# One matmul instead of three between the sixth and the seventh product of a Strassen step

## The chip, the cores and the metric

The kernel runs on one core of a Trainium2 chip. The metric is the time of one execution in microseconds (us) on the device. Three runs of the kernel before took 2034.97, 2035.05 and 2035.65 us, so the median is 2035.05 us. One further execution was profiled; the trace and all views quoted below are of that one.

## The reference

The program is a decoder trunk of two layers over 256 positions and 2048 channels, in float32:

```python
for l in range(DEPTH):                                   # 2
    h = rms_norm(x, norm1_g[l])
    z = h @ w_in[l]                                      # 2048 x 5120
    q, k, v, gu, gv = jnp.split(z, splits, axis=-1)
    attn = dilated_attention(rotary(q), rotary(k), v)    # 8 heads
    gm = chunked_gmlp(gelu(gu), gelu(gv), ...)           # 8 groups
    x = x + concatenate([attn, gm]) @ w_out[l]           # 2048 x 2048
    h2 = rms_norm(x, norm2_g[l])
    x = x + square(relu(h2 @ w_up[l])) @ w_down[l]       # 2048 x 8192 x 2048
return rms_norm(x, final_g)
```

The change lies in the last product, `w_down`, and in the steps that stand among its own.

## The kernel before, in words

**Precision.** Every large product is made of three matmuls in a float32 form with a short mantissa. A weight block `raw` is split into `hi` (a rounded copy, made by ScalarE, L167) and `lo` (what the rounding left, `raw - hi`, made by VectorE, L177). The activations are split the same way. A product is then `hi*xh + lo*xh + hi*xl`. So a block of weights can be used by its first matmul once ScalarE has made `hi`, and by its second once VectorE has made `lo`.

**Steps.** The work is a list of steps, and each consumes one or more weight blocks of 128 x 1024 numbers. There are three kinds:

- `natural`: the activations are the stationary operand and 512 weight columns stream (lines 459 to 461).
- `transposed`, the channel-major step: the weights are stationary and 256 positions stream. One step is one block: 2 column halves times 4 row blocks times the three matmuls of lines 400 (`hi`, `xh`), 402 (`lo`, `xh`) and 404 (`hi`, `xl`), so 24 matmuls. Its output goes to a PSUM bank `acc`.
- `fast`, the seven-product step: a Strassen-like multiplication of 2 x 2 blocks with seven products in place of eight, used on a part of `w_down`. Here 128 x 128 pieces of the activations (`half`, or their sums in `shared`) are stationary and 256 weight columns stream. A product is 2 times the three matmuls of lines 430 (`hi`), 432 (`lo`) and 433 (`hi` with the low part of the activations), so 6 matmuls. A step takes four blocks, two of the weights themselves (`Top`, `Bottom`) and two of their sums (`Sums`, first `upper`, then `lower`); the sums are made by VectorE in four subtractions (L218, L219, L222, L223), and then these blocks are split into `hi` and `lo` as the others are. The last `lo` of the four is that of `lower`.

**The seventh product.** The step issues six products and puts the seventh into the list `left_over`. The next step is always a `transposed` one. Within it, ahead of the second row block, the seventh product is taken from the list and issued: so behind the first three matmuls of that step. It writes its own half of a PSUM bank `aux`. It uses the `lower` block, which the sixth product has used already, and the activations in `half`.

**Order.** The program is written step by step and the order on each engine is the order of the code. Before the matmuls of a step the loop at the end of the kernel writes the `hi` of later blocks for ScalarE, the due pieces of earlier results, the `lo` of later blocks for VectorE, and the loads. VectorE works in that order too, so its `lo` for one step stands behind the sums, the other splits and the accumulations written ahead of it.

**How often.** For each of the eighths `e = 1` to `7` of the hidden width, the tables `ORDER` and `USUAL` give the places of two or three column groups of 512, each with two seven-product steps: 2 + 3 + 3 + 3 + 3 + 3 + 2 = 19 groups in a layer, 38 steps, and 76 in both layers. So there are 76 places at which a seventh product is issued inside a `transposed` step.

Of the kernel before, what the change touches and what calls it, by code (L numbers as in the profile page):

```python
# [90 lines left out]
def trunk(ctx: ExitStack, tc: tile.TileContext, layout, xT, consts, gains, w, b_sp, w_sp, out):  # L91
# [42 lines left out]
    def acc_bank(i=None, of=4):  # L134

        if i is None:
            i = bank_at[0] = (bank_at[0] + 1) % of
        return pacc.tile([P, 512], F32, name=f"acc{i}", tag=f"acc{i}")
# [217 lines left out]
    left_over = []  # L356
# [12 lines left out]
    def transposed(name, l, row0, nk, col0, ncols, moving, after, between=None, apart=False, of=4, cols=None):  # L369

        cols = cols or range(0, ncols, 256)
        order = [(c, k) for c in cols for k in range(0, nk, 4)]
        if between:
            h = nk // 8
            order[h:2 * h], order[2 * h:3 * h] = order[2 * h:3 * h], order[h:2 * h]  # L380
        accs = {}
        for n, (c, k0) in enumerate(order):
            if between and n == nk // 4:
                mark(between)
            wt = Sub(name, l, row0 + k0 * P, col0 + c, 4, 256)

            def mm(wt=wt, k0=k0, c=c):
                two = apart and c == cols[-1]
                if k0 == 0:
                    accs[c] = [acc_bank(of=of), acc_bank(of=of)] if two else acc_bank(of=of)  # L390
                ps = accs[c]
                for cb in range(2):
                    o = ps[cb][:, 0:S] if two else ps[:, cb * S:(cb + 1) * S]
                    for k in range(4):
                        if cb == 0 and k == 1 and left_over:
                            left_over.pop()()
                        xs = moving(k0 + k)
                        hi = wt.hi[:, k, cb * P:(cb + 1) * P]
                        last = k0 + k == nk - 1
                        pe.matmul(o, lhsT=hi, rhs=xs[:, 0, :], start=(k0 + k == 0 and (two or cb == 0)), stop=False,  # L400
                                  skip_group_check=True)
                        pe.matmul(o, lhsT=wt.lo[:, k, cb * P:(cb + 1) * P], rhs=xs[:, 0, :], start=False, stop=False,  # L402
                                  skip_group_check=True)
                        pe.matmul(o, lhsT=hi, rhs=xs[:, 1, :], start=False, stop=last, skip_group_check=True)  # L404
            steps.append((wt, mm, (lambda c=c: after(c, accs[c])) if k0 + 4 == nk else None))
# [58 lines left out]
    def mark(fn):  # L464

        steps.append((None, fn, None))
# [601 lines left out]
```

## Time and profile before

| | before |
|---|---|
| median of three runs | 2035.05 us (2034.97 to 2035.65) |
| profiled execution, first to last instruction (its span) | 2033.3 us |
| TensorE matmul busy | 2018.3 us (99%), 16834 matmuls |
| VectorE busy | 1577.6 us (78%) |
| ScalarE busy | 1213.4 us (60%) |
| granted TensorE clock, mean | 0.997 |

The profile gives no other time for the profiled execution than its span; the median of the runs is 1.75 us longer than the span, for what lies ahead of the first and behind the last instruction.

How to read the rows that follow. In a row of the timeline stand the start, the duration, the engine, the line, the operation and the tiles (written `out<-in`). PE is TensorE's matmul, PEld its weight load, DVE is VectorE, ACT is ScalarE. Matmuls are pipelined: each lasts about 0.28 us in the records and the next begins about 0.113 us after it, so what counts is the distance from one start to the next, not the duration. In a row of waits stand who waited for whom, the microseconds in total, how many times, and the longest.

### The profile page before, as it was taken

Reading aid. Unit: us, or ns where it says so; the run is one execution under the profiler, and the core shown is the slowest. Engines: PE = TensorE matmul, PEld = TensorE weight load, DVE = VectorE, ACT = ScalarE, POOL = GpSimd, SP = SyncE. Lnnn points to the kernel's source line nnn. Section 1 sums busy time; section 2 is a strip of 40 time slices with the busy share of each in tenths; the row PEclk is TensorE's granted clock in tenths of the full one; section 3 lists DMA queues with packets and bytes.
Section 4 is the critical chain, followed back from the end, with each engine's and each line's share of the span. In section 5 each row is a group of like instructions: output and inputs, shape, how many; then the busy total and the mean of one; then the engine's idle time right before and its main releaser. Section 6 shows DMA issues by size and latency. Waiting matters only on the chain.

```text
span 2033.3 us, 40721 instructions
## 1 busy us (share of the span) xinstructions
PE 2018.3 (99%) x16834; PEld 1979.1 (97%) x16834; DVE 1577.6 (78%) x1950; ACT 1213.4 (60%) x1613; POOL 156.7 (8%) x200
## 2 busy tenths in 40 slices
PE   9999999999999999999999999999999999999997
PEld 8998999999999999999989989999999999999997
DVE  7566766688888898998856667667888898888985
ACT  7565454666666666656545654556666666667654
POOL 0002300000001001100000032000000100010000
PEclk9999999999999999999999999999999999999998
DMA  8555556566677766875664555565676776778562
GB/s 326 192 167 166 187 187 205 169 232 209 211 228 236 244 218 201 243 222 198 204 214 159 169 184 187 187 203 179 215 223 213 230 234 217 230 221 261 184 213 81
DMA packets 126443, 419.27 MB, mean 206 GB/s; under 512 B 14128, under 2 KB 22064, under 8 KB 126256
## 3 DMA queue, kind: packets, MB, share of 16 engines
q1 hardware_dynamic: 110800, 389.86, 56.4%
q0 software_dynamic: 14304, 23.86, 6.7%
q8 instruction: 132, 2.16, 0.4%
q10 hardware_dynamic: 1152, 2.94, 0.4%
q14 instruction: 55, 0.45, 0.1%
HBM read 394.58 MB, written 22.02 MB: 205 GB/s over the span
## 4 chain that ended last, share of the span: by engine, by line
PE 95%; DVE 3%; ACT 1%; issue 1%; DMA 1%; ACTq 0%; DVEq 0%; SPq 0%
PE acc L402 23%; PE acc L400 23%; PE acc L404 23%; PE acc L461 3%; PE acc L460 3%; PE acc L459 3%; PE aux L430 3%; PE aux L432 3%; PE acc L433 3%; PE aux L433 3%; PE acc L432 3%; PE acc L430 3%; DVE lo L177 1%; ACT hi L167 1%; PE aux L693 0%
## 5 line engine op out<-in xcount | busy, mean ns | idle before, releaser
L167 ACT ACTIVATE hi<-raw 128x1024 fp32r<-128x1024 f32 (+1 forms) x817 | 836.2, 1051 | 497.9 <-DVE raw L219 231.2
L177 DVE TENSOR_TENSOR lo<-raw,hi 128x1024 fp32r<-128x1024 f32 (+1 forms) x817 | 964.1, 1213 | 155.1 <-ACT hi L167 151.7
L400 PE MATMUL acc<-hs,hi 128*128 128x256 f32 x2816 | 781.3, 277 | 0.0
L402 PE MATMUL acc<-hs,lo 128*128 128x256 f32 x2816 | 779.4, 277 | 0.2
L404 PE MATMUL acc<-hs,hi 128*128 128x256 f32 x2816 | 778.3, 276 | 0.0
L402 PEld LDWEIGHTS acc<-hs,lo 128*128 128x128 f32 x2816 | 528.7, 188 | 2.5 <-DVE lo L177 1.8
L400 PEld LDWEIGHTS acc<-hs,hi 128*128 128x128 f32 x2816 | 528.7, 188 | 0.3 <-issue 0.2
L404 PEld LDWEIGHTS acc<-hs,hi 128*128 128x128 f32 x2816 | 528.6, 188 | 0.0
L400 PE MATMUL acc<-half,hi 128*128 128x256 f32 x1344 | 372.1, 277 | 2.3 <-ACT hi L167 2.3
L402 PE MATMUL acc<-half,lo 128*128 128x256 f32 x1344 | 371.0, 276 | 0.0
L404 PE MATMUL acc<-half,hi 128*128 128x256 f32 x1344 | 371.0, 276 | 0.0
L400 PEld LDWEIGHTS acc<-half,hi 128*128 128x128 f32 x1344 | 252.3, 188 | 2.6 <-ACT hi L167 2.6
L402 PEld LDWEIGHTS acc<-half,lo 128*128 128x128 f32 x1344 | 252.3, 188 | 0.0
L404 PEld LDWEIGHTS acc<-half,hi 128*128 128x128 f32 x1344 | 252.2, 188 | 0.0
L866 POOL DMA_DIRECT2D far<-ar x92 | 74.7, 983 | 1159.9 <-ACT ar L869 607.0
L432 PE MATMUL acc<-lo,shared 128*128 128x256 f32 x384 | 106.4, 277 | 0.0
L433 PE MATMUL acc<-hi,shared 128*128 128x256 f32 x384 | 106.1, 276 | 0.0
L430 PE MATMUL acc<-hi,shared 128*128 128x256 f32 x384 | 106.1, 276 | 0.0
L459 PE MATMUL acc<-hi,hs 128*128 128x512 f32 x256 | 101.5, 397 | 0.1
L461 PE MATMUL acc<-hi,hs 128*128 128x512 f32 x256 | 100.6, 393 | 0.0
L460 PE MATMUL acc<-lo,hs 128*128 128x512 f32 x256 | 100.1, 391 | 0.3 <-DVE lo L177 0.3
L643 DVE TENSOR_TENSOR half<-ar,half 128x512 fp32r<-128x512 f32 x72 | 49.7, 691 | 62.1 <-ACT half L640 61.0
(163 smaller groups left out, 2560.2 us busy)
## 6 DMA issues: line engine op xcount, KB each, us to landing
raw<-in_w SPq DMA_DIRECT2D x731, 512.0 KB, 4.7
far<-ar POOLq DMA_DIRECT2D x60, 256.0 KB, 6.0
far<-ar POOLq DMA_DIRECT2D x32, 128.0 KB, 4.5
ar<-far POOLq DMA_DIRECT2D x12, 256.0 KB, 8.6
raw<-in_w SPq DMA_DIRECT2D x10, 256.0 KB, 5.2
x<-in_xT SPq DMA_DIRECT2D x7, 256.0 KB, 5.6
out<-x SPq DMA_DIRECT2D x7, 256.0 KB, 3.1
shared<-in_b_sp ACTq DMA_DIRECT2D x2, 512.0 KB, 7.8
```

The lines of the kernel that those rows point to most:

```text
L167: act.activation(self.h[:, j * m:(j + 1) * m], self.raw[:, j * m:(j + 1) * m], AF.Copy)
L177: vec.tensor_tensor(lo[:, r], self.raw[:, r], self.h[:, r].bitcast(F32), op=OP.subtract)
L400: pe.matmul(o, lhsT=hi, rhs=xs[:, 0, :], start=(k0 + k == 0 and (two or cb == 0)), stop=False, skip_group_check=True)
L402: pe.matmul(o, lhsT=wt.lo[:, k, cb * P:(cb + 1) * P], rhs=xs[:, 0, :], start=False, stop=False, skip_group_check=True)
L404: pe.matmul(o, lhsT=hi, rhs=xs[:, 1, :], start=False, stop=last, skip_group_check=True)
L430: pe.matmul(o[n], lhsT=xh, rhs=hi, start=(p == 0 and k == 0 and n in fresh), stop=False, skip_group_check=True)
L432: pe.matmul(o[n], lhsT=xh, rhs=lo, start=False, stop=False, skip_group_check=True)
L433: pe.matmul(o[n], lhsT=xl, rhs=hi, start=False, stop=(n in last and p == 1 and k == 1), skip_group_check=True)
L459: pe.matmul(ps, lhsT=xh, rhs=hi, start=(k0 + k == 0), stop=False)
L460: pe.matmul(ps, lhsT=xh, rhs=lo, start=False, stop=False)
L461: pe.matmul(ps, lhsT=xl, rhs=hi, start=False, stop=(k0 + k == KC - 1))
L866: nc.gpsimd.dma_start(far[g][:, r], src, **({} if e == max(g, 1) else {"accum_op": OP.add}))
```

## The change

The diff moves the two lines that take the seventh product from the list. They stood ahead of a row block's three matmuls, on condition that it is the second of the first half; they stand now behind the first of the three, wherever the list is not empty. As the list is filled by the step just before, that is the first matmul of the step.

```diff
                 for cb in range(2):
                     o = ps[cb][:, 0:S] if two else ps[:, cb * S:(cb + 1) * S]
                     for k in range(4):
-                        if cb == 0 and k == 1 and left_over:
-                            left_over.pop()()
                         xs = moving(k0 + k)
                         hi = wt.hi[:, k, cb * P:(cb + 1) * P]
                         last = k0 + k == nk - 1
                         pe.matmul(o, lhsT=hi, rhs=xs[:, 0, :], start=(k0 + k == 0 and (two or cb == 0)), stop=False,
                                   skip_group_check=True)
+                        if left_over:
+                            left_over.pop()()
                         pe.matmul(o, lhsT=wt.lo[:, k, cb * P:(cb + 1) * P], rhs=xs[:, 0, :], start=False, stop=False,
                                   skip_group_check=True)
                         pe.matmul(o, lhsT=hi, rhs=xs[:, 1, :], start=False, stop=last, skip_group_check=True)
```

With the two lines gone from above it, the first of the three matmuls moves from line 400 to line 398; 402 and 404 keep their numbers.

On TensorE, at the first of the 76 places (the end of the first seven-product step of `e = 1` in layer 0; `hi_4437` and `lo_4469` are the block of the `transposed` step, `hi_4407` and `lo_4439` that of `lower`), the order before is:

```order
L433 MATMUL aux_4475<-hi_4407,shared_4236 128x256
L400 MATMUL acc0_4382<-hs_85,hi_4437 128x256 [waits Activation_49]
L402 MATMUL acc0_4382<-hs_85,lo_4469 128x256 [waits DVE_49]
L404 MATMUL acc0_4382<-hs_85,hi_4437 128x256
L430 MATMUL aux_4476<-hi_4407,half_3857 128x256
L432 MATMUL aux_4476<-lo_4439,half_3857 128x256
L433 MATMUL aux_4476<-hi_4407,half_3857 128x256
L430 MATMUL aux_4476<-hi_4407,half_3857 128x256
L432 MATMUL aux_4476<-lo_4439,half_3857 128x256
L433 MATMUL aux_4476<-hi_4407,half_3857 128x256
L400 MATMUL acc0_4382<-hs_85,hi_4437 128x256
```

Now it is:

```order
L433 MATMUL aux_4475<-hi_4407,shared_4236 128x256
L398 MATMUL acc0_4382<-hs_85,hi_4437 128x256 [waits Activation_49]
L430 MATMUL aux_4476<-hi_4407,half_3857 128x256
L432 MATMUL aux_4476<-lo_4439,half_3857 128x256
L433 MATMUL aux_4476<-hi_4407,half_3857 128x256
L430 MATMUL aux_4476<-hi_4407,half_3857 128x256
L432 MATMUL aux_4476<-lo_4439,half_3857 128x256
L433 MATMUL aux_4476<-hi_4407,half_3857 128x256
L402 MATMUL acc0_4382<-hs_85,lo_4469 128x256 [waits DVE_49]
L404 MATMUL acc0_4382<-hs_85,hi_4437 128x256
L398 MATMUL acc0_4382<-hs_85,hi_4437 128x256
```

The six matmuls of the seventh product moved ahead of the step's second and third matmul. The wait for VectorE's `lo` went with the second matmul, six places back; the wait for ScalarE's `hi` stayed. The six themselves wait for nothing in either order.

The second place is the second seven-product step of the column group that the table puts at places 1 and 2 of `e = 6`, in layer 0 (`hi_9612` and `lo_9654` are the block of the `transposed` step, `hi_9610` and `lo_9616` that of `lower`). Before:

```order
L433 MATMUL acc0_9561<-hi_9610,shared_4236 128x256
L400 MATMUL acc1_9527<-hs_85,hi_9612 128x256 [waits Activation_49]
L402 MATMUL acc1_9527<-hs_85,lo_9654 128x256 [waits DVE_49]
L404 MATMUL acc1_9527<-hs_85,hi_9612 128x256
L430 MATMUL aux_4476<-hi_9610,half_8722 128x256
L432 MATMUL aux_4476<-lo_9616,half_8722 128x256
```

Now:

```order
L433 MATMUL acc0_9561<-hi_9610,shared_4236 128x256
L398 MATMUL acc1_9527<-hs_85,hi_9612 128x256 [waits Activation_49]
L430 MATMUL aux_4476<-hi_9610,half_8722 128x256
L432 MATMUL aux_4476<-lo_9616,half_8722 128x256
L433 MATMUL aux_4476<-hi_9610,half_8722 128x256
L430 MATMUL aux_4476<-hi_9610,half_8722 128x256
L432 MATMUL aux_4476<-lo_9616,half_8722 128x256
L433 MATMUL aux_4476<-hi_9610,half_8722 128x256
L402 MATMUL acc1_9527<-hs_85,lo_9654 128x256 [waits DVE_49]
```

It is the same move, and no wait is added or dropped. The orders of VectorE, ScalarE, GpSimd and SyncE are the same in both kernels, instruction for instruction, so no load and no store moves against them.

## Prediction

> **What bounds the kernel now.** I read the page first, then the waits of TensorE, then the order of time around the places that the change touches.
>
> ```profile
> span 2033.3 us, 40721 instructions
> PE 2018.3 (99%) x16834; PEld 1979.1 (97%) x16834; DVE 1577.6 (78%) x1950; ACT 1213.4 (60%) x1613; POOL 156.7 (8%) x200
> PEld acc L400 <- ACT hi L167: 2.6, 2, 1.3
> PEld acc L402 <- DVE lo L177: 1.8, 8, 0.3
> ```
>
> TensorE sets the time, and it hardly stands still. The last two rows are from the waits of its weight loads, with total, count and longest: in the whole span only 1.8 us go to a channel-major step's second matmul (L402) waiting for VectorE's `lo`. This is the wait that the change moves, so the gain cannot be large. Now the places in order of time, TensorE's matmuls alone:
>
> ```profile
> 802.22 0.28 PE L400 MATMUL acc<-hs,hi 128*128 128x256 f32 x1
> 802.51 0.39 PE L402 MATMUL acc<-hs,lo 128*128 128x256 f32 x1
> 802.73 0.28 PE L404 MATMUL acc<-hs,hi 128*128 128x256 f32 x1
> ...
> 808.26 0.28 PE L432 MATMUL acc<-lo,shared 128*128 128x256 f32 x1
> ...
> 810.27 0.28 PE L400 MATMUL acc<-hs,hi 128*128 128x256 f32 x1
> 810.60 0.39 PE L402 MATMUL acc<-hs,lo 128*128 128x256 f32 x1
> 810.83 0.28 PE L404 MATMUL acc<-hs,hi 128*128 128x256 f32 x1
> ...
> 893.05 0.28 PE L430 MATMUL acc<-hi,shared 128*128 128x256 f32 x1
> 893.22 0.39 PE L432 MATMUL acc<-lo,shared 128*128 128x256 f32 x1
> 893.45 0.28 PE L433 MATMUL acc<-hi,shared 128*128 128x256 f32 x1
> ...
> 924.31 0.28 PE L400 MATMUL acc<-hs,hi 128*128 128x256 f32 x1
> 924.54 0.39 PE L402 MATMUL acc<-hs,lo 128*128 128x256 f32 x1
> 924.76 0.28 PE L404 MATMUL acc<-hs,hi 128*128 128x256 f32 x1
> ...
> 1930.51 0.28 PE L400 MATMUL acc<-hs,hi 128*128 128x256 f32 x1
> 1930.73 0.39 PE L402 MATMUL acc<-hs,lo 128*128 128x256 f32 x1
> 1930.95 0.28 PE L404 MATMUL acc<-hs,hi 128*128 128x256 f32 x1
> ```
>
> From the first row of a triple to the third are two gaps, which take 0.23 us at the usual 0.113. They take 0.51 at 802, so 0.28 are lost there; 0.56 at 810, so 0.33; 0.45 at 924, so 0.22; 0.44 at 1930, so 0.21. I count ten such places in the trace: the pair 802 and 810 stands four times (twice in each layer, at the seven-product steps that follow each other closely in `e = 6` and in `e = 7`), and 924 and 1930 are the same step in the two layers. The triple at 893 is another wait, inside a seven-product step between the two of such a pair: 0.40 for two gaps, so 0.17 lost. The change does not touch that one.
>
> What VectorE does meanwhile:
>
> ```profile
> 800.10 2.35 DVE L177 TENSOR_TENSOR lo<-raw,hi 128x1024 fp32r<-128x1024 f32 x2
> 802.37 0.68 DVE L190 TENSOR_TENSOR lo<-raw,hi 128x512 fp32r<-128x512 f32 x1
> ...
> 806.28 0.69 DVE L223 TENSOR_TENSOR raw<-raw 128x512 f32<-128x512 f32 x1
> 806.89 4.79 DVE L177 TENSOR_TENSOR lo<-raw,hi 128x1024 fp32r<-128x1024 f32 x4
> ...
> 802.00:812.00 10.00, 9.50 (x11) 1.00 0.63 190
> ...
> 1951.78 0.69 DVE L782 SCALAR_TENSOR_TENSOR ar<-acc,nR 128x512 f32<-128x512 f32 x1 [3.12 <-PE acc L404]
> ```
>
> In the window from 802 to 812 it is busy 9.50 of 10.00 us (fifth row), without a pause until 806.89 + 4.79 = 811.68. In these stretches VectorE does not follow TensorE; it is late from its own queue. Outside them it does: the last row has it idle for 3.12 us until TensorE delivers, in layer 1 behind all 76 places, and a gain made before such a row is kept.
>
> **The ordinary place.** At the 66 others no wait is to be seen, but the pace is:
>
> ```profile
> 400.59 0.28 PE L433 MATMUL aux<-hi,shared 128*128 128x256 f32 x1
> 400.70 0.28 PE L400 MATMUL acc<-hs,hi 128*128 128x256 f32 x1
> 400.82 0.28 PE L402 MATMUL acc<-hs,lo 128*128 128x256 f32 x1
> 400.94 0.28 PE L404 MATMUL acc<-hs,hi 128*128 128x256 f32 x1
> 401.06 0.28 PE L430 MATMUL aux<-hi,half 128*128 128x256 f32 x1
> 401.18 0.28 PE L432 MATMUL aux<-lo,half 128*128 128x256 f32 x1
> ...
> 401.77 0.28 PE L400 MATMUL acc<-hs,hi 128*128 128x256 f32 x1
> 401.89 0.28 PE L402 MATMUL acc<-hs,lo 128*128 128x256 f32 x1
> ...
> 402.12 0.28 PE L400 MATMUL acc<-hs,hi 128*128 128x256 f32 x1
> ...
> L430 PE MATMUL aux<-hi,half x264: 276/280/283, 396.6 to 1931.4; 128*128 128x256 f32 x132
> L430 PE MATMUL aux<-hi,shared x224: 276/276/277, 398.0 to 1930.2; 128*128 128x256 f32 x112
> ```
>
> From 400.59 to 402.12 are 13 gaps, 1.53 us, where 13 x 0.1133 = 1.47 would do: about 0.057 lost. The gap into the step is normal (0.11). From the gap behind its first matmul on, each is 0.117 to 0.122, through the three matmuls, the six of the seventh product and two more. The last two rows, from the view of line 430 (shortest, median, longest ns), say that this is so everywhere: of the 264 matmuls on `aux` and `half` 152 are seventh products, and their group's median is 280 ns; where the same line runs deep inside a step (`aux` and `shared`) it is 276 with at most 277. So 76 x 0.057 = 4.3 us hang on changing between the two kinds of step.
>
> **The change, part by part.** No instruction is added or removed; on the other engines nothing moves. At each place six matmuls come ahead of two.
>
> *The moved wait.* Behind the waiting L402 stood the seventh product, which needs nothing new. It now covers the wait with six gaps, 6 x 0.113 = 0.68 us, more than the longest loss of 0.33. Behind the wait now stands only the rest of its own step. So at all ten places the stall there ends. What is late next:
>
> - At 924 and 1930 nothing close follows. Gain 0.22 + 0.21 = 0.43.
> - In a pair, the first stall's gain is not kept. TensorE would reach the seven-product step's wait 0.28 us earlier, at 893.22 in the second pair and 808.26 in the first. At 893 it waits already. At 808.26 the `lo` it needs is the first of the four that begin at 806.89, done at 806.89 + 4.79/4 = 808.09, and a weight load starts a gap ahead of its matmul, at 808.15: nothing to spare. As VectorE has no pause there, TensorE waits those 0.28 us at that place. Gain 0. If VectorE did move with TensorE, it would be the whole 4 x 0.28 = 1.1.
> - The second stall's gain is kept, since VectorE is through at 811.68. Gain 4 x 0.33 = 1.3.
>
> *The slow pace.* After 1930 it lasts longer than elsewhere:
>
> ```profile
> 925.50:930.50 5.00, 5.00 (x47) 1.00 0.87 304
> 1931.50:1936.50 5.00, 5.00 (x45) 1.00 0.87 281
> ```
>
> In equal 5 us two matmuls fewer are done in layer 1, at 0.113 about 0.2 us. It set in with the stall; without the stall I count it as gained: 0.2.
>
> At each place the stretch of slow gaps loses two members, since two matmuls of the step no longer stand between the first switch and the seventh product. At 0.005 each that is 0.010, times 76 = 0.8. The trace has no switch after a single matmul, so this has two ends: the stretch vanishes (0.057, gain 4.3), or it outlives the step (rival 2, loss). I take the value that goes by the rows as they are: six slow gaps of the seventh product, and two behind.
>
> A rule of the Trainium skill bears on this term: the page "TensorE: Matmul & The Clock Gate", section "Step-by-step: what each phase is for", says that TensorE has two SBUF read ports, so that loading the next weights takes no bandwidth from the running matmul. By it the kind of step before or behind would cost nothing, the place of the seventh product would not matter to the pace, and this term would be 0 and the whole gain 1.9 us. The trace does not show it so: 0.12 against 0.113 at every switch back to a channel-major step.
>
> **Sum.** 0.43 + 0 + 1.3 + 0.2 + 0.8 = 2.7 us, off the profiled span of 2033.3 us: 2030.6. The runs' median is 1.75 us above that span and nothing in what lies around it changes, so 2035.05 - 2.7 = **2032.4 us**. The likeliest case's own range is 2031.3 (with the first stalls' 1.1 too) to 2033.5 (without the pace's 0.8 and the 0.2).
>
> **Rivals.** 0.2% of the time is 4.1 us, which is about what a measurement of this kernel can tell from no change; faster means below 2031.0, slower above 2039.1.
>
> 1. *The slow pace goes altogether.* One matmul is too short for it to set in: in the rows it is seen first behind the first matmul of the step, and the gap at 400.59 is normal. Then the 0.8 becomes 4.3, the sum 6.2 and the time 2028.8. Against it: the gap from 400.70 to 400.82, which still exists, is slow already.
> 2. *The slow pace no longer ends.* This is the one on the other side. In the rows it ends two gaps behind the second switch back, at 401.77 to 402.12; but after 1930 it did not end for 5 us, with the same matmuls in the same order. If with one matmul between the switches it lasted to the end of the step at every place, some 22 more gaps of 0.005, that would be 0.11 x 76 = 8.4 us, against 1.9 gained: 2041.5. Above 0.025 us a place it eats the gain; above 0.08 the kernel is slower by over 0.2%. For it: at ten places with a disturbed start one is seen to behave so. Against it: the 66 others all end the same way.
> 3. *VectorE takes it all back.* The four second stalls and those at 924 and 1930 return at the next `lo`, since VectorE is the late one: gain 0 to 0.8, time 2034.7. For it: 9.50 of 10.00 us busy. Against it: the pause behind 811.68, and no further wait for `lo` of this size in the list of waits.
>
> That the change does not do what it says I exclude: the order shows the wait six places further back.
>
> **How the numbers follow.** The forecast has 0.60, rival 1 has 0.15 (not always in full), rival 2 has 0.12, rival 3 has 0.13. The range of 2029.6 to 2036.2 holds the forecast, rival 3, the lesser forms of rival 1 and the mild ones of rival 2, and leaves out about 0.2. Faster by over 0.2%: 0.16, rival 1 and a little of the forecast. Slower: 0.09, rival 2 without its mild forms. Within 0.2%: 0.75.
>
> **What would show it.** In the list of waits of the weight loads, L402 for `lo` goes from 1.8 us in 8 to nothing, and L432 for `lo`, which is missing in it now, appears with four waits of some 0.2 to 0.4 (the loads' own idle time, which is less than what the gaps lose). At 893 the two gaps rise from 0.40 to about 0.7. The 13 gaps of the ordinary place take 1.52 instead of 1.53; 1.47 would be rival 1, and a pace of 0.118 that runs on into the step rival 2. If L402 still waits, the cover of 0.68 us is not what I think it is; if TensorE does not wait at 808 and 893, VectorE did follow it, and the gain is 1.1 larger.

## The result

The changed kernel takes 2043.12 us (median of 5 runs, 2042.54 to 2043.97) against 2035.05 us of the kernel before (5 runs, 2034.77 to 2035.65): a ratio of 1.0041 with the interval 1.0030 to 1.0051. It is 8.1 us slower. The forecast was 2032.4 us, the range 2029.6 to 2036.2.

The page of the profile after, and of the waits of its weight loads the only row for a `lo` of these steps:

```profile
span 2041.5 us, 40721 instructions
PE 2027.1 (99%) x16834; PEld 1989.5 (97%) x16834; DVE 1577.9 (77%) x1950; ACT 1213.7 (59%) x1613; POOL 157.2 (8%) x200
...
PEld acc L432 <- DVE lo L177: 0.9, 4, 0.2
```

TensorE is as busy as before, only longer, by 8.2 us of span. The wait of L402 that the change moved is gone from the list (it was 1.8 us, 8 times), and L432 has its four waits. The timeline of TensorE's matmuls at the first close pair shows both, and no loss but these:

```profile
806.56 0.28 PE L398 MATMUL acc<-hs,hi 128*128 128x256 f32 x1
806.68 0.28 PE L430 MATMUL aux<-hi,half 128*128 128x256 f32 x1
...
807.38 0.28 PE L402 MATMUL acc<-hs,lo 128*128 128x256 f32 x1
807.50 0.28 PE L404 MATMUL acc<-hs,hi 128*128 128x256 f32 x1
...
812.21 0.28 PE L430 MATMUL acc<-hi,shared 128*128 128x256 f32 x1
812.52 0.39 PE L432 MATMUL acc<-lo,shared 128*128 128x256 f32 x1
```

L402 starts at the pace of its neighbours (0.12 to the next), where the kernel before lost 0.28 us at this place. Further on, within the next seven-product step, TensorE waits 0.2 us for a `lo`, as was forecast. So the stalls went as they should, and 10 us came from elsewhere. The ordinary places show from where. First the end of the first and then of the second seven-product step of `e = 1`, again TensorE's matmuls in order of time:

```profile
401.21 0.28 PE L433 MATMUL aux<-hi,shared 128*128 128x256 f32 x1
401.32 0.28 PE L398 MATMUL acc<-hs,hi 128*128 128x256 f32 x1
401.44 0.28 PE L430 MATMUL aux<-hi,half 128*128 128x256 f32 x1
401.56 0.28 PE L432 MATMUL aux<-lo,half 128*128 128x256 f32 x1
...
402.03 0.28 PE L433 MATMUL aux<-hi,half 128*128 128x256 f32 x1
402.14 0.28 PE L402 MATMUL acc<-hs,lo 128*128 128x256 f32 x1
402.26 0.28 PE L404 MATMUL acc<-hs,hi 128*128 128x256 f32 x1
402.38 0.28 PE L398 MATMUL acc<-hs,hi 128*128 128x256 f32 x1
...
414.63 0.28 PE L433 MATMUL aux<-hi,shared 128*128 128x256 f32 x1
414.75 0.28 PE L398 MATMUL acc<-hs,hi 128*128 128x256 f32 x1
...
415.57 0.29 PE L402 MATMUL acc<-hs,lo 128*128 128x256 f32 x1
415.69 0.28 PE L404 MATMUL acc<-hs,hi 128*128 128x256 f32 x1
415.81 0.28 PE L398 MATMUL acc<-hs,hi 128*128 128x256 f32 x1
415.93 0.28 PE L402 MATMUL acc<-hs,lo 128*128 128x256 f32 x1
416.04 0.28 PE L404 MATMUL acc<-hs,hi 128*128 128x256 f32 x1
416.15 0.28 PE L398 MATMUL acc<-hs,hi 128*128 128x256 f32 x1
...
427.60 0.28 PE L433 MATMUL acc<-hi,shared 128*128 128x256 f32 x1
```

The first place is entered at the fast pace (0.11 from 401.21 to 401.32) and left at the slow one, which goes on; the second is entered slow (0.12 from 414.63) and left fast, the last two gaps at 416 being 0.11 again. The cost is best read from one row to the next of the same kind. L433 at 401.21, 414.63 and 427.60 is the last matmul of the sixth product at three successive places, with the same work between. In the kernel before, where the first such row stands at 400.59, the next two are:

```profile
413.57 0.28 PE L433 MATMUL aux<-hi,shared 128*128 128x256 f32 x1
426.55 0.28 PE L433 MATMUL acc<-hi,shared 128*128 128x256 f32 x1
```

From the first to the second place it took 12.98 us and takes 13.42 now; from the second to the third 12.98, and 12.97 now. I took the 75 distances between the 76 such rows in both traces. The 38 that begin at a first place of a group are longer by 9.5 us in sum (0.23, 0.34 or 0.44 us each, by their length, outside the close pairs). The 37 that begin at a second place are shorter by 1.3 us in sum, of which the second stalls of three of the four close pairs are 0.32 to 0.33 each; behind the fourth the pace stayed slow and it is 0.23 longer. Together that is the 8.2 us of the span; the first of these rows stands 0.62 us later than before and what follows the last is 0.67 shorter, which all but cancels.

So the pace of TensorE has two states, about 0.113 and 0.118 us for a matmul with its weight load, and each keeps itself. In the changed kernel the first place of a group turns it slow and the second turns it back. The exception is the end of the trace: in the last close pair the pace is fast again behind the stall inside the seven-product step, and from there the last three places do it the other way round. At the ordinary places no instruction waits in between. The granted clock is 0.998 against 0.997 over the whole run, and in the stretch from 403 to 413 us it is 1.00 in both traces, with 88 matmuls now and 90 before.

### The profile page after: what moved, and what is told of

Read it like the earlier page. It is cut to its first block, busy times and chain, and to the rows that moved or that the text cites. A ratio compares the mean times of both kernels' runs of the same rounds, so it can differ in the third digit from the quotient of the medians.

```text
span 2041.5 us, 40721 instructions
## 1 busy us (share of the span) xinstructions
PE 2027.1 (99%) x16834; PEld 1989.5 (97%) x16834; DVE 1577.9 (77%) x1950; ACT 1213.7 (59%) x1613; POOL 157.2 (8%) x200
## 4 chain that ended last, share of the span: by engine, by line
PE 99%; DVE 0%; ACT 0%; issue 0%; DVEq 0%
PE acc L404 23%; PE acc L398 23%; PE acc L402 23%; PE acc L432 3%; PE acc L430 3%; PE acc L433 3%; PE acc L461 3%; PE acc L459 3%; PE acc L460 3%; PE aux L430 3%; PE aux L433 3%; PE aux L432 3%; PE aux L693 0%; PE aux L587 0%; PE aux L629 0%; PE aux L616 0%
## 5 line engine op out<-in xcount | busy, mean ns | idle before, releaser
L402 PE MATMUL acc<-hs,lo 128*128 128x256 f32 x2816 | 780.2, 277 | 0.0
L402 PEld LDWEIGHTS acc<-hs,lo 128*128 128x128 f32 x2816 | 530.7, 188 | 0.4 <-issue 0.2
L402 PE MATMUL acc<-half,lo 128*128 128x256 f32 x1344 | 371.0, 276 | 0.0
L402 PEld LDWEIGHTS acc<-half,lo 128*128 128x128 f32 x1344 | 252.3, 188 | 0.0
L432 PE MATMUL acc<-lo,shared 128*128 128x256 f32 x384 | 107.0, 279 | 0.1
L433 PE MATMUL acc<-hi,shared 128*128 128x256 f32 x384 | 106.6, 278 | 0.0
```

Of the source, the lines that this page charges most:

```text
L432: pe.matmul(o[n], lhsT=xh, rhs=lo, start=False, stop=False, skip_group_check=True)
L433: pe.matmul(o[n], lhsT=xl, rhs=hi, start=False, stop=(n in last and p == 1 and k == 1), skip_group_check=True)
```

## The experiments

Each was timed beside the kernel before on the same chip. "Switch back" below is a switch from a product's matmuls to those of the channel-major step. The place distances are read from the last matmul of the sixth product, as above.

### Is it the number of matmuls ahead, or the wait behind the switch?

Four orders were run together. The first puts the seventh product behind two matmuls (shown against the changed kernel; the diffs of the others are cut to the lines that matter):

```diff
-                        if left_over:
-                            left_over.pop()()
                         pe.matmul(o, lhsT=wt.lo[:, k, cb * P:(cb + 1) * P], rhs=xs[:, 0, :], start=False, stop=False,
                                   skip_group_check=True)
+                        if left_over:
+                            left_over.pop()()
```

> The seventh product behind two matmuls of the channel-major step (hi, lo), so that the wait for lo stands ahead of it again and no wait stands behind the second switch back. Theory A (number of matmuls: one or two between the two switches are too few for the pace to recover at the second one): slow pace of about 0.118 us from one seven-product step of a group to the next, as in the changed kernel, and the ten stalls for lo back: 2043 to 2046 us. Theory B (the wait: a wait for lo right behind the second switch back keeps the pace slow): none stands there, so the pace recovers as in the kernel before, 2035 us within 1.

Measured: 2035.45 us against 2034.95, ratio 1.0002 (0.9992 to 1.0011). The first two places and the wait for `lo`:

```profile
401.08 0.28 PE L433 MATMUL aux<-hi,shared 128*128 128x256 f32 x1
414.05 0.28 PE L433 MATMUL aux<-hi,shared 128*128 128x256 f32 x1
...
PEld acc L400 <- DVE lo L177: 1.9, 8, 0.3
```

12.97 us, the fast pace, with the stalls back (line 400 is the `lo` matmul here). Two matmuls between the switches are enough, so Theory A's count is wrong at least for two. This speaks for the wait.

The second has three matmuls ahead that need `hi` alone, so that the wait for `lo` comes behind the second switch:

```diff
-                    for k in range(4):
-                        if cb == 0 and k == 1 and left_over:
+                    kinds = "hxhllx" if cb == 0 and left_over else "hlxhlx"
+                    for n, kind in enumerate(kinds + "hlxhlx"):    # h: hi*xh, l: lo*xh, x: hi*xl
+                        if cb == 0 and n == 3 and left_over:
                             left_over.pop()()
```

> Three matmuls ahead of the seventh product as in the kernel before, but the three that need hi alone; the wait for lo stands right behind the second switch back, as in the changed kernel. Theory A (number): the pace recovers at each place, and the stalls for lo are gone: about 2033 us (2035.05 less the 1.9 of the forecast). Theory B (wait): slow from place to place as in the changed kernel, 2043 us.

Measured: 2039.37 us, ratio 1.0020 (1.0011 to 1.0030), between the two. The trace tells more than the time:

```profile
400.55 0.28 PE L437 MATMUL aux<-hi,shared 128*128 128x256 f32 x1
413.53 0.28 PE L437 MATMUL aux<-hi,shared 128*128 128x256 f32 x1
...
810.11 0.28 PE L437 MATMUL acc<-hi,shared 128*128 128x256 f32 x1
826.34 0.28 PE L437 MATMUL acc<-hi,shared 128*128 128x256 f32 x1
```

At the first place the distance is 12.98 us as in the kernel before, although the wait stands behind the switch; 60 of the 76 places are left fast. Theory B falls. From 810.11 to 826.34 it is 16.23 us (16.02 in the kernel before, with its stall): there the stall within the seven-product step has made the pace slow, the places that follow are entered slow and left slow, 16 in all.

The third has none ahead (`k == 0` in place of `k == 1` in the condition of the kernel before):

> The seventh product right behind the sixth: one switch back in place of two, with the waits for hi and lo behind it. Theory A (number): nothing is left between two switches; the one switch costs what that from the input projection's matmuls does in the profile before (four slow gaps, about 0.016 us in place of 0.057), and the stalls for lo are covered: 2035.05 - 1.9 - 76 x 0.041 = 2030 us. Theory B (wait): the wait for lo stands as close behind the switch as anywhere, slow pace, 2043 us or more.

Measured: 2042.46 us, ratio 1.0037 (1.0024 to 1.0050).

```profile
400.51 0.28 PE L433 MATMUL aux<-hi,shared 128*128 128x256 f32 x1
413.91 0.28 PE L433 MATMUL aux<-hi,shared 128*128 128x256 f32 x1
426.88 0.28 PE L433 MATMUL acc<-hi,shared 128*128 128x256 f32 x1
```

13.40 us and then 12.97: with a single switch back, every first place turns the pace slow and every second fast, 38 of each. Theory A falls too; no wait is needed and nothing is too close together.

The fourth has six ahead (`k == 2`):

> The seventh product behind six matmuls of the channel-major step. The wait for lo stands ahead of it, the stalls are there. Theory A (number): six are enough for the pace to recover between the switches and again behind the second; about 0.03 to 0.06 us at each place as before, 2035 us within 1.5. Theory B (wait): no wait behind the second switch, 2035 us as well. This run does not tell A from B; it tells whether the position alone, without parity or closeness, brings the slow pace: if it does, 2040 us or more, both fall.

Measured: 2041.05 us, ratio 1.0030 (1.0019 to 1.0041). By what I had written both theories fall with it, but the time does not mean what I had meant:

```profile
400.69 0.28 PE L433 MATMUL aux<-hi,shared 128*128 128x256 f32 x1
413.68 0.28 PE L433 MATMUL aux<-hi,shared 128*128 128x256 f32 x1
```

12.99 us; at 57 of the 76 places the pace is fast before and behind. The loss is nearly all around the close pairs of `e = 6` and `e = 7`, as in the run with three `hi` ahead: the pace becomes slow at a stall and the places behind do not change it.

**A new theory.** What fits all four, with the kernels before and after, at the places without a stall: every switch back turns the pace over, from fast to slow and from slow to fast. None ahead is one switch a place, so it alternates; two, three and six are two, so a place leaves the pace as it came, be that fast or slow. A single matmul ahead counts as one, not two. I call this Theory C. The second steps of the four close pairs, which are entered slow and have a stall of 0.33 us at the first switch, do not follow it throughout. In the kernel before, with two switches, all four are left fast; with six ahead, also two switches, all four are left slow; with two ahead three are left fast and one slow.

### Theory C tested

The change at the first step of each group alone (`p` is the number of the step in its group):

```diff
-                left_over.append(lambda: product(6, half, 1, 1, lower, left))
+                left_over.append((p, lambda: product(6, half, 1, 1, lower, left)))
...
                         pe.matmul(o, lhsT=hi, rhs=xs[:, 0, :], ...)
+                        if left_over and left_over[0][0] == 0:
+                            left_over.pop()[1]()
```

> The change at the first seven-product step of each column group alone; at the second one the seventh product stays behind three matmuls as before. Theory C (every switch back from a product to channel-major matmuls flips the pace between 0.113 and 0.118, and after a single matmul the two switches of a place count as one): the place with the change leaves the pace flipped, the other (two flips) leaves it as it came, so the slow pace runs from the first step of one group to that of the next and is fast in every other such stretch. From the times of these places in the profile before that is some 260 us of slow pace a layer, at 0.0045 in 0.113 about 10 us a layer: 2055 us, worse than the whole change. Theory A (a changed place brings its own slow stretch, and the next place ends it): at most the stretches of the changed kernel, 2043 us or less.

Measured: 2050.06 us against 2035.27, ratio 1.0076 (1.0059 to 1.0093). Half of the change costs nearly twice as much as the whole.

```profile
400.68 0.28 PE L435 MATMUL aux<-hi,shared 128*128 128x256 f32 x1
414.11 0.28 PE L435 MATMUL aux<-hi,shared 128*128 128x256 f32 x1
427.51 0.28 PE L435 MATMUL acc<-hi,shared 128*128 128x256 f32 x1
```

13.43 and 13.40: the second place, which has two switches, leaves the slow pace as it is, and only the next group's first place ends it. Theory A's 2043 or less is excluded. Theory C's 2055 is 5 us too high, although the slow stretches of this trace add up to 522 us, the 260 a layer that it took. Most of the difference is probably that the kernel before already loses its 0.057 us at each place, 4.3 us in all, which the estimate did not take off.

Next, what the switch is made of. At the switch back the weight loads take weight blocks while the last product matmul still streams one. A matmul that adds zero was put between (with none ahead):

```diff
+        def neutral(to):
+            pe.matmul(to, lhsT=zeros[:, 0:1].to_broadcast([P, P]), rhs=hs[:, 0, 0, :], start=False, stop=False, ...)
...
-                left_over.append(lambda: product(6, half, 1, 1, lower, left))
+                left_over.append(lambda: (product(6, half, 1, 1, lower, left), neutral(o[6])))
```

> None ahead as in the run before with that order, and between the seventh product and the channel-major step one more matmul that adds zero to the seventh product's output: its stationary operand is a column of zeros, its moving operand the activations that the channel-major step streams. So no weight load of weight blocks stands beside a matmul that streams weight blocks. Theory O (the flip comes from that overlap): no flip, fast pace throughout: 2035.05 less 1.9 (stalls) and 4.3 (slow gaps), more 76 x 0.113 for the added matmuls, about 2037.5 us. Theory K (the flip comes with leaving the product's matmuls, whatever stands between): 38 slow stretches as with none ahead, 2042.5 + 8.6 = 2051 us.

Measured: 2054.46 us, ratio 1.0095 (1.0080 to 1.0110).

```profile
403.91 0.28 PE L437 MATMUL aux<-hi,shared 128*128 128x256 f32 x1
417.43 0.28 PE L437 MATMUL aux<-hi,shared 128*128 128x256 f32 x1
430.50 0.28 PE L437 MATMUL acc<-hi,shared 128*128 128x256 f32 x1
```

13.52 and 13.07: again every place turns the pace over. In 34 groups the first place turns it slow and the second fast; in the four groups of `e = 7` it is the other way round, as the pace came slow to the first of them, from a turn at four small matmuls at 879.3 us (and likewise in layer 1). The overlap is not the cause; Theory K holds. The time is 3 us above its 2051, and the rows show where: the first place stands at 403.91 in this execution, where that of the kernel before stands at 400.59. The 3.3 us are lost ahead of any seventh product, where TensorE ran at the slow pace from 59 us on (96 matmuls from 109.5 to 120.5 us, against 98 from 107 to 118 in the kernel before). Why it did so here is open.

Then two kernels that use the theory. In the first, the seventh product is split, five of its matmuls ahead and the sixth behind two `hi` matmuls, so that a place has two switches close together; the four second steps of the close pairs, entered slow because of a stall, have one:

```diff
+                        if cb == 0 and left_over and n in (0, 2):    # kinds "hxlhlx" at such a place
+                            left_over.pop()()
...
-                left_over.append(lambda: product(6, half, 1, 1, lower, left))
+                seventh = [lambda r=r: product(6, half, 1, 1, lower, left, r)
+                           for r in ((range(6),) if late and p == 1 else (range(5), range(5, 6)))]
+                left_over.extend(reversed(seventh))
```

(`product` takes the numbers of the matmuls to issue; `late` is true for the group at places 1 and 2.)

> Five of the seventh product's six matmuls right behind the sixth product, two hi matmuls of the channel-major step, then the last of the six, then the rest; at the four second steps of the close pairs in the sixth and seventh eighth (where a stall within the step has brought the slow pace) all six right behind, so one switch. Theory C: two flips at the 72 places, one at the four, fast pace everywhere outside the places, the slow stretch at a place shortened from 11 gaps to about 5, and the stalls for lo covered: 2035.05 - 1.9 - 72 x 0.03 = 2031 us. If a single product matmul doesn't count as a switch, each place has one flip: 2042 us.

Measured: 2033.40 us against 2035.27, ratio 0.9990 (0.9981 to 0.9999), faster than the kernel before. All 72 split places are entered and left fast, and a single product matmul counts as a switch. The slow stretch at such a place has 8 gaps, though, not 5, and the time is above the 2031 of Theory C. It was run again:

> The kernel with the split seventh product once more, for a narrower interval: 2033.4 us measured against 2035.3 of the kernel before; 0.998 to 1.000 of it again.

Measured: 2032.64 us against 2034.95, ratio 0.9985 (0.9976 to 0.9994). It is the fastest kernel of this study, and its rows serve for the stalls. The first pair, before and in this kernel:

```profile
802.11 0.28 PE L433 MATMUL acc<-hi,shared 128*128 128x256 f32 x1
810.15 0.28 PE L433 MATMUL acc<-hi,shared 128*128 128x256 f32 x1
826.17 0.28 PE L433 MATMUL acc<-hi,shared 128*128 128x256 f32 x1
```

```profile
801.76 0.28 PE L441 MATMUL acc<-hi,shared 128*128 128x256 f32 x1
809.82 0.28 PE L441 MATMUL acc<-hi,shared 128*128 128x256 f32 x1
825.50 0.28 PE L441 MATMUL acc<-hi,shared 128*128 128x256 f32 x1
```

Over the first stall 8.04 us became 8.06, over the second 16.02 became 15.68: the first gives nothing, the second 0.34.

The same repair with three `hi` ahead at the other places:

```diff
+                        if cb == 0 and left_over and n == (0 if left_over[0][0] else 3):
+                            left_over.pop()[1]()
...
+                left_over.append((late and p == 1, lambda: product(6, half, 1, 1, lower, left)))
```

> Three hi matmuls ahead of the seventh product as in the run with that order, but none ahead at the four second steps of the close pairs, which the slow pace enters because of the stall for lo within the step. Theory C: the one flip there sets the pace back to fast, so the 16 slow places of that run go, and what stays is the gain of the covered stalls: 2033 us, faster than the kernel before. If the flip is not what ends a slow pace, it stays at 2039 us.

Measured: 2035.05 us against 2035.27, ratio 0.9997 (0.9987 to 1.0006), with runs from 2033.3 to 2038.0. Between the two expectations: in the profiled execution three of the four repaired places are left fast, and one is entered and left slow, with the places behind it (810.27 to 826.53 in these rows):

```profile
810.27 0.28 PE L437 MATMUL acc<-hi,shared 128*128 128x256 f32 x1
826.53 0.28 PE L437 MATMUL acc<-hi,shared 128*128 128x256 f32 x1
```

So the single switch is not wholly sure behind a stall. What decides there I do not know.

Last, the change itself kept, with one further switch added to every place (five of the six behind the first matmul, the sixth behind the third; one piece at the four late places, as in the split kernel):

```diff
-                        if cb == 0 and left_over and n in (0, 2):
+                        if cb == 0 and left_over and n in (1, 3):    # kinds "hlxhlx" again
```

> The change kept, and one more switch back added to each place: one matmul of the channel-major step (hi), five of the seventh product's six, two of the channel-major step (lo, hi), the last of the six, the rest. At the four second steps of the close pairs the last is not held back, so that these are as in the changed kernel. Theory C with its rule for the single matmul (a place with one matmul ahead flips the pace once in all): the further switch makes it two, the 37 slow stretches of the changed kernel go, and what stays is the gain of the covered stalls: 2033 to 2034 us. If a single matmul ahead gave two flips and something else made the changed kernel slow, three flips leave the slow pace: 2043 us or more. If the changed kernel's loss has nothing to do with the pace, it stays at 2043 us.

Measured: 2033.77 us against 2034.95, ratio 0.9990 (0.9981 to 0.9999).

```profile
400.34 0.28 PE L441 MATMUL aux<-hi,shared 128*128 128x256 f32 x1
413.32 0.28 PE L441 MATMUL aux<-hi,shared 128*128 128x256 f32 x1
426.30 0.28 PE L441 MATMUL acc<-hi,shared 128*128 128x256 f32 x1
```

12.98 and 12.98. The single matmul ahead is still there, the wait for `lo` still stands behind the switch, and the loss of 8 us has turned into a gain of 1.2. This run shows that the loss came from the pace, and that a place with a single matmul ahead turns it over once.

## Why the prediction was wrong

- *The moved wait* held, term by term. The ten stalls of L402 are gone. The first stall of a pair gives 0 and returns as a wait of the seven-product step (8.04 against 8.06 us in the split kernel); the second gives 0.32 to 0.34 (in the split kernel at all four pairs), forecast 0.33. VectorE did not follow TensorE in these stretches, as the argument from its rows had it.
- *The slow pace* is the step that failed. It was put down as a stretch that starts at a switch and has a length, so that two matmuls fewer in it were a gain of 0.010 a place, 0.8 in sum. In the traces it is a state that a switch back turns over. In the second half of a group the changed kernel does gain that 0.010 (12.98 to 12.97). In the first half the slow state is not ended at its own place and costs 0.23 to 0.44 us until the next, outside the close pairs; the first halves lose 9.5 us in sum.
- The end of the stretch was read wrongly for the same reason: "it ends two gaps behind the second switch back" was taken as a length that always runs out. At the ordinary places it was the second switch that ended it; with one matmul between them the two switches act as one, and nothing is left to end it.
- Rival 2 had the sign and nearly the size (2041.5 against 2043.1) at a chance of 0.12. That the size came so near is luck: it took 76 stretches to the end of a step, and the runs have 38 longer ones. Its pointer, the 5 us of slow pace behind 1930, was the right one. Its form was off: not every place with a slow rest of its step, but every other place with a slow stretch until the next. The argument against it, that 66 places all end the same way, was worth little: they were all of the same order, and the order is what was changed.
- One end of the likeliest case's own range is mis-added: without the pace's 0.8 and the 0.2 the sum leaves 2033.3 us, not 2033.5. Nothing hangs on it.
- The Trainium skill's rule of two read ports ("TensorE: Matmul & The Clock Gate", "Step-by-step: what each phase is for") would have had the place of the seventh product make no difference to the pace; the runs show one of 10 us. The run with the neutral matmul shows that it does not take a stream of weight blocks beside a load of weight blocks at the switch: with that matmul between them the pace turned over as well.
- The trace of the kernel before held a second stretch like that behind 1930, which the prediction passed over ("at ten places with a disturbed start one is seen to behave so"). Behind the stall at 802 the pace stays slow up to the next place at 810, while behind the same stall in layer 1 it does not. The same stretch of work, with the number of TensorE's matmuls in brackets:

```profile
803.70:807.90 4.20, 4.20 (x38) 1.00 0.55 192
1809.90:1814.10 4.20, 4.20 (x40) 1.00 0.56 194
```

Two paces for the same matmuls in the same order, each lasting: this was the sign of a state rather than a length.

## What to carry to other kernels

Where a trace shows two paces for the same instruction, ask what ends the slow one and not only what begins it, and mark at each place the pace before and the pace behind: a rearrangement that shortens a slow stretch can take away its end. Where an edit is made at many equal places, look at two places in a row and at the distance between the same rows, since the cost may fall on the stretch between them. An average over all places would have hidden it here: 0.44 at one, nothing at the next.

## What the runs showed of the hardware

TensorE ran matmuls of 256 columns, each with its own weight load of 128, at 0.1133 or at 0.1178 us from start to start with the clock granted in full (1.00 in the windows of both paces), and stayed at the slow one for 124 matmuls in a row in the changed kernel (401.32 to 415.93). A change from a product's matmuls (activations stationary, 256 weight columns streaming) to channel-major ones (weights stationary) turned the pace over; the change the other way did not: with none ahead, 13.40 and 12.97 us alternate, and each step has one change of either kind. Two such changes back with one channel-major matmul between them worked as one, with two, three or six as two; a run of a single product matmul was enough for a change of its own.

This does not hold for every such change of operands, nor are these changes the only thing that turns the pace. The change from the `natural` steps (512 columns) to channel-major ones at 198.4 us of the kernel before gave four slow gaps and then the fast pace. Small matmuls between channel-major steps turned it too: in the kernel before the 24 channel-major matmuls from 338.85 to 341.64 us, between two groups of small ones, ran at the slow pace with no product near, and in the run with three `hi` ahead four small matmuls at 876.29 us ended a slow stretch. A stall for a semaphore could leave either pace. What in the engine holds the pace, why one matmul is too short, and what decides behind a stall stays open; no run here told these apart.
